# Modulation weights, and output weights for the samples' rows, multiplied as unsplit float32, four tiles in a row in four column groups

## The chip, the cores and the metric

The kernel runs on one core of a Trainium2 chip. A time is the device time of one execution in microseconds (us); the run before gave 2041.84 us as the median of three, from 2039.24 to 2042.91. The profile is of one further execution, of 2031.15 us. The engines are named as in its rows: PE (TensorE, matmuls), PEld (its weight loads), DVE (VectorE), ACT (ScalarE), POOL (GpSimd), SP (the queue that issues the transfers).

## The reference, cut to what matters

One layer of a streaming encoder is applied to a prompt of 1024 rows and to a sample of 32 rows, with 2048 channels. Two products matter here:

```python
shift, scale, gate = jnp.split(c @ w_mod + b_mod, 3, axis=-1)   # c: one row for the prompt, one for the sample
u = layer_norm(x) * (1.0 + scale[:, None]) + shift[:, None]
...                                                             # w_in, four branches of heads
o = jnp.concatenate([y_a, y_b, y_c, y_d], axis=-1) @ w_out      # 2048 x 2048
x_new = layer_norm(ALPHA * x + (1.0 + gate[:, None]) * o) * ln_g + ln_b
```

`c @ w_mod` has two rows, over a matrix of 2048 x 4096 for scale and shift. `@ w_out` has 1024 prompt rows and 32 sample rows.

## The kernel before, in words

Large products are made of float32 numbers split in two: a rounded high part (`float32r`, ACT's copy) and the rest (DVE's subtraction). A product is then three matmuls: high by high, high by low, low by high. The matmuls that take float32 as it is appear in the trace as two rows of PE each.

**Modulation.** `mod_group(g, part)` computes 512 of the columns of scale (part 1) or shift (part 0): 16 tiles `wmr` of 128x512 (256 KB each) are loaded, ACT casts each to `wmh` (L206), DVE subtracts (L207; POOL takes every fifth), and PE multiplies `wmh` by `cspl`, four columns that hold the high and the low parts of the two rows of `c` (L208), and `wml` by two of them (L209), all into one PSUM tile `mod`. DVE copies that tile (`mr`, L213), and four small matmuls (L215) add the rows that belong together and turn them into columns. Of eight such groups the first four (part 1) come first, since the scaled input `u` needs them: `build_u0` makes 16 tiles `uh`, `ul` from the transposed, normalised `x` (L273 to L279). The other four run woven with four column tiles of the input projection (`col_tile`, L337 to L339), which need `u`.

**The samples' rows in the output projection.** `out_proj(0)` handles the first 512 prompt rows and the 32 sample rows, in four blocks of 512 output columns. For each block eight weight tiles `wr` (2 of the 16 k each, 512 KB) are loaded (L308, two buffers), cast and subtracted to `wh`, `wl` (L312, L313, three buffers each). 24 matmuls of 512 columns multiply them by the prompt rows (`product`, L1218 to L1220). Then four matmuls (L1262, L1263) multiply the same `wh`, `wl` by the sample rows `ys` into `accs`. `so` (L1273) and one matmul (L1275) add the parts.

A scheduler fixes the order of each engine's instructions when the program is built; `tc.high_priority()` marks work that it puts as early as it can. Within an engine's queue, and in SP's, instructions are taken in that order.

Two other places serve as comparisons. `products` multiplies two heads j = 0, 1, which lie in partitions 0 to 63 and 64 to 127, so that their matmuls use different rows of the array. `values` multiplies unsplit float32 and puts the two heads in output partitions 0 to 63 and 64 to 127, that is in two column groups of the array:

```python
T.matmul(out, x[0], y[0], start=start, stop=False)      # products(), L716, called for j = 0, then for j = 1
T.matmul(out, x[0], y[1], start=False, stop=False)      # L717
T.matmul(out, x[1], y[0], start=False, stop=stop)       # L718
...
for j in range(2):                                       # values(), L829
    T.matmul(pa[64 * j:64 * j + 64, 0:P], vv[:, b * P + 64 * j:b * P + 64 * j + 64],
             wt[:, j * P:(j + 1) * P], start=first and b == 0, stop=last and b == m // P - 1,
             skip_group_check=True)
```

Of the kernel before, what the change touches and what calls it, by code (L numbers as in the profile page):

```python
# [62 lines left out]
def step_kernel(ctx, tc, xp, xs, cst, wmss, wmg, bgate, win, wsm, wout, lng, lnb, ck, cv,  # L63
# [72 lines left out]
    for sel, (s0, s1) in ((sel1, (0, 16)), (sel2, (32, 48))):  # L136
# [12 lines left out]
    A.activation(mulc, C("ral"), AF.Exp)  # L149
    V.tensor_scalar(mulc, mulc, -1.0, None, op0=ALU.mult)  # L150

    cspl = cp.tile([P, KD, 4], F32R, name="cspl")
    cT = g4(C("cT", 0, 32), KD)
    A.copy(cspl[:, :, 0:2], cT)
    V.tensor_tensor(cspl[:, :, 2:4], cT, cspl[:, :, 0:2].bitcast(F32), op=ALU.subtract)
    sel4 = cp.tile([4, 2], F32, name="sel4")
    tmp4 = cp.tile([4, 2], F32, name="tmp4")
    G.affine_select(out=sel4, in_=ones[0:4, 0:2], pattern=[[-1, 2]], compare_op=ALU.is_equal,
                    fill=0.0, base=0, channel_multiplier=1)
    G.affine_select(out=tmp4, in_=ones[0:4, 0:2], pattern=[[-1, 2]], compare_op=ALU.is_equal,  # L160
                    fill=0.0, base=-2, channel_multiplier=1)
    G.tensor_tensor(sel4, sel4, tmp4, op=ALU.add)


    mhi = cp.tile([6, 1], F32, name="mhi")
# [5 lines left out]
    sel32 = cp.tile([64, 32], F32, name="sel32")  # L171
    G.tensor_tensor(sel32, ident[0:64, 0:32], ident[0:64, 32:64], op=ALU.add)


    shiftH = cp.tile([P, KD, 2], F32R, name="shiftH")
# [19 lines left out]
    usc = dp.tile([KD, P, 512], F32, name="usc")  # L195
    gpk = [dp.tile([4, P, 544], F32, name=f"gpk{h}") for h in range(2)]


    def mod_group(g, part):
        o = ZT("mod")  # L200
        for kk in range(KD):
            wr = IO("wmr")
            nc.sync.dma_start(wr[:, 0:512], wmss[g, kk, part])
            wh = wk.tile([P, 512], F32R, tag="wk", name=nm("wmh"))
            wl = wk.tile([P, 512], F32R, tag="wk", name=nm("wml"))
            A.copy(wh, wr[:, 0:512])  # L206
            (G if kk % 5 == 4 else V).tensor_tensor(wl, wr[:, 0:512], wh.bitcast(F32), op=ALU.subtract)  # L207
            T.matmul(o[0:4], cspl[:, kk, :], wh, start=(kk == 0), stop=False, skip_group_check=True)  # L208
            T.matmul(o[0:2], cspl[:, kk, 0:2], wl, start=False, stop=(kk == KD - 1), skip_group_check=True)  # L209
            yield 1  # L210
        pc = ST("modc")
        mr = WK("mr")
        V.tensor_copy(mr[0:4, 0:512], o[0:4])  # L213
        for j in range(4):
            T.matmul(pc[:, 2 * j:2 * j + 2], mr[0:4, j * P:(j + 1) * P], sel4, start=True, stop=True)  # L215
        ks = slice(4 * g, 4 * g + 4)
        if part == 1:
            V.scalar_tensor_tensor(scale1[:, ks, :], g4(pc[:, 0:8], 4), 1.0,
                                   C("bmod", 16 + 4 * g, 4).to_broadcast([P, 4, 2]), op0=ALU.add, op1=ALU.add)
        else:  # L220
            sh = SM(8, "shf")
            V.tensor_tensor(g4(sh, 4), g4(pc[:, 0:8], 4), C("bmod", 4 * g, 4).to_broadcast([P, 4, 2]), op=ALU.add)
            V.tensor_copy(shiftH[:, ks, :], g4(sh, 4))
# [81 lines left out]
    def split_w(src, shape, pool=None):  # L305

        wr = wp.tile(shape, F32, tag="wr", name=nm("wr"), bufs=2)
        nc.sync.dma_start(wr, src)  # L308
        p, th, tl = (pool, "io", "io") if pool else (wp, "wh", "wl")
        wh = p.tile(shape, F32R, tag=th, name=nm("wh"))  # L310
        wl = p.tile(shape, F32R, tag=tl, name=nm("wl"))
        A.copy(wh, wr)  # L312
        V.tensor_tensor(wl, wr, wh.bitcast(F32), op=ALU.subtract)  # L313
        return wh, wl

    def spans(h, shift):

# [4 lines left out]
    def col_tile(h, tid, shift=None):  # L322

        if shift is None:
            shift = h == 0
        src = win[tid]
        with tc.high_priority():
            w = [split_w(src[:, q * 1024:(q + 1) * 1024].rearrange("p (a b) -> p a b", a=8), [P, 8, P])
                 for q in range(2)]
        res = []  # L330
        sp_ = spans(h, shift)
        for i, (c0, t0, o, n) in enumerate(sp_):
            pt = ps_ip.tile([P, 512], F32, tag="ip", name=nm("ip"))
            for k in range(KD):
                uh, ul = U[h, k]
                wh, wl = w[k // 8]
# [820 lines left out]
    def load_y(h, k):  # L1157
# [12 lines left out]
        A.copy(yh[:, 0:n], yf[:, 0:n])  # L1170
        V.tensor_tensor(yl[:, 0:n], yf[:, 0:n], yh[:, 0:n].bitcast(F32), op=ALU.subtract)
        if h == 0:
            if k % 8 == 0:
                YS[k // 8] = io.tile([P, 8, 64], F32R, tag="io", name=nm("ys2"))
            t = YS[k // 8]
            G.tensor_copy(t[:, k % 8, 0:32], yh[:, 512:544].bitcast(F32))
            G.tensor_copy(t[:, k % 8, 32:64], yl[:, 512:544].bitcast(F32))
        Y[h, k] = (yh, yl)

    def row_norm(st, m):  # L1180
# [9 lines left out]
    def out_proj(h):  # L1190
# [4 lines left out]
        for c0, w in blocks:  # L1195
# [12 lines left out]
            def weights(k0, n, pool=None):  # L1208
                src = wout[b, k0 // 4, :, :].rearrange("p (a b) -> p a b", a=4)[:, k0 % 4:k0 % 4 + n, o:o + w]
                with tc.high_priority():  # L1210
                    wh, wl = split_w(src, [P, n, w], pool)
                return [(k0 + i, wh[:, i, :], wl[:, i, :]) for i in range(n)]

            def product(t, ws, first, last):
                c = slice(t * P, (t + 1) * P)
# [38 lines left out]
            for kq in range(KD // nk):  # L1254
                ws = weights(kq * nk, nk)
                for t in range(4):
                    product(t, ws, kq == 0, kq == KD // nk - 1)
                if h == 0:
# [6 lines left out]
                    if b == 3:  # L1265
                        for k, _, _ in ws:
                            load_y(1, k)
                yield 1
            for t in range(4):
                residual(t, P, xp, h * 512 + t * P, acc[t][:, 0:w], gb[0])  # L1270
            if h == 0:
                so = WK("so")
                A.copy(so[0:64, 0:512], accs[0:64])  # L1273
                pt = ST("pso")
                T.matmul(pt[0:SMP, :], sel32[0:64], so[0:64, 0:512], start=True, stop=True)  # L1275
                residual(4, SMP, xs, 0, pt[0:SMP, :], gb[1])

    def finish0():
# [266 lines left out]
```

## Time and profile before

| | |
|---|---|
| median of three runs | 2041.84 us (2039.24 to 2042.91) |
| profiled execution | 2031.15 us |
| its span, first to last instruction | 2029.3 us |
| PE busy | 1941.8 us (96%) |
| DVE busy | 1426.9 us (70%) |
| ACT busy | 836.1 us (41%) |
| mean granted TensorE clock | 0.994 of full speed |

The span is what the rows below divide; 1.9 us of the profiled execution lie outside it. Matmuls overlap in the pipeline, so a matmul's own duration is longer than the time by which it holds back the next one: what a matmul costs is read from the starts of rows that follow each other.

### The profile page before, as it was taken

The page shows a single profiled execution, that of the slowest core. Times are in us where ns is not written, and L with a number is a line of the kernel's source. Part 1 is how long each engine was busy: PE and PEld are TensorE (multiplying, and loading weights), DVE is VectorE, ACT ScalarE, POOL GpSimd, SP SyncE. Part 2 cuts the span into 40 slices and gives each one's busy share as a digit, 9 for nine tenths or more (in the row PEclk, how much of TensorE's full clock was granted, in tenths as well). Part 3 has the DMA queues.
Part 4 walks back from the last instruction along what each step waited for, and adds up shares of the span by engine and source line. Part 5 has one row for each costly group of instructions (what it writes and reads, how often), then busy time and mean ns, then how long its engine had stood idle before and what let it go on. Part 6 is the DMA issues. An engine that isn't in the chain of part 4 may idle for free.

```text
span 2029.3 us, 31738 instructions
## 1 busy us (share of the span) xinstructions
PE 1941.8 (96%) x11820; PEld 1625.0 (80%) x11820; DVE 1426.9 (70%) x2713; ACT 836.1 (41%) x1407; POOL 323.8 (16%) x521
## 2 busy tenths in 40 slices
PE   2999999999999999999999999999999999999998
PEld 0568999998889999987787877777778777777787
DVE  6976558779776776877669797886757754356765
ACT  6663443333545434444444443534335521133321
POOL 1232011122121311241101010111102410000000
PEclk9999999999999999999999999999999999999999
DMA  9785334443444334364232333233342725468733
GB/s 306 250 281 185 107 119 131 127 137 102 139 132 137 110 106 120 85 204 141 91 114 95 119 92 108 82 110 113 106 120 92 224 94 168 128 224 261 229 126 130
DMA packets 162034, 291.40 MB, mean 144 GB/s; under 512 B 23836, under 2 KB 66076, under 8 KB 161880
## 3 DMA queue, kind: packets, MB, share of 16 engines
q1 hardware_dynamic: 161880, 289.37, 45.0%
q8 instruction: 93, 1.52, 0.3%
q14 instruction: 61, 0.50, 0.1%
HBM read 253.49 MB, written 35.82 MB: 143 GB/s over the span
## 4 chain that ended last, share of the span: by engine, by line
PE 53%; DVE 11%; DMA 4%; issue 4%; POOL 1%; ACT 1%; SPq 0%; POOLq 0%; DVEq 0%; ACTq 0%
PE ip L337 10%; PE ip L339 10%; PE ip L338 10%; PE op L1220 5%; PE op L1219 4%; PE op L1218 4%; DVE cv L1089 3%; DVE wl L313 2%; DMA val<-rsc 1%; DVE pr L697 1%; DMA wg<-in_wmg_dram 1%; PE av L829 1%; PE wt L814 1%; DVE gacc L1142 1%; ACT wh L312 1%
## 5 line engine op out<-in xcount | busy, mean ns | idle before, releaser
L337 PE MATMUL ip<-uh,wh 128*128 128x272 f32 (+4 forms) x2368 | 774.0, 328 | 0.6 <-DVE uh L278 0.6
L338 PE MATMUL ip<-ul,wh 128*128 128x272 f32 (+4 forms) x2368 | 764.6, 323 | 0.2
L339 PE MATMUL ip<-uh,wl 128*128 128x272 f32 (+4 forms) x2368 | 763.0, 322 | 0.0
L312 ACT CAST wh<-wr 128x1024 fp32r<-128x1024 f32 (+1 forms) x257 | 268.3, 1045 | 658.0 <-PE ip L338 379.8
L337 PEld LDWEIGHTS ip<-uh,wh 128*128 128x128 f32 x2368 | 449.2, 190 | 39.1 <-issue 5.5
L313 DVE TENSOR_TENSOR wl<-wr,wh 128x1024 fp32r<-128x1024 f32 (+1 forms) x257 | 315.0, 1226 | 233.7 <-ACT wh L312 221.7
L338 PEld LDWEIGHTS ip<-ul,wh 128*128 128x128 f32 x2368 | 450.1, 190 | 34.4 <-issue 2.4
L339 PEld LDWEIGHTS ip<-uh,wl 128*128 128x128 f32 x2368 | 449.8, 190 | 34.4 <-issue 2.0
L1218 PE MATMUL op<-wh,yh 128*128 128x512 f32 (+1 forms) x576 | 214.0, 372 | 3.1 <-DVE val L1229 3.1
L1219 PE MATMUL op<-wl,yh 128*128 128x512 f32 (+1 forms) x576 | 213.4, 371 | 0.0
L1220 PE MATMUL op<-wh,yl 128*128 128x512 f32 (+1 forms) x576 | 212.6, 370 | 0.0
L1089 DVE SCALAR_TENSOR_TENSOR cv<-cin,cs,cv 128x574 f32<-128x574 f32 (+1 forms) x240 | 187.5, 781 | 2.9
L1218 PEld LDWEIGHTS op<-wh,yh 128*128 128x128 f32 x576 | 108.3, 188 | 26.7 <-DVE val L1229 4.0
L1219 PEld LDWEIGHTS op<-wl,yh 128*128 128x128 f32 x576 | 108.3, 188 | 22.0 <-issue 2.6
L1220 PEld LDWEIGHTS op<-wh,yl 128*128 128x128 f32 x576 | 108.3, 188 | 20.8 <-issue 1.3
L790 POOL TENSOR_SCALAR_AFFINE_SELECT s<-s 128x128 f32<-128x128 f32 x64 | 36.3, 568 | 430.2 <-ACT s L688 430.0
L1142 DVE SCALAR_TENSOR_TENSOR gacc<-wg,cs,gacc 128x512 f32<-128x512 f32 x120 | 89.2, 760 | 17.7 <-DMA wg<-in_wmg_dram 17.4
L208 PE MATMUL mod<-wmh,cspl 128*4 128x512 f32 x128 | 52.9, 413 | 34.6 <-ACT wmh L206 34.5
L207 DVE TENSOR_TENSOR wml<-wmr,wmh 128x512 fp32r<-128x512 f32 x104 | 78.9, 812 | 3.9 <-ACT wmh L206 3.2
L206 ACT CAST wmh<-wmr 128x512 fp32r<-128x512 f32 x128 | 71.0, 621 | 15.4 <-PE modc L215 10.3
L697 DVE TENSOR_TENSOR_SCAN pr<-kp 128x128 f32<-128x128 f32 (+4 forms) x66 | 54.0, 818 | 14.4 <-POOL kp L792 11.7
L688 ACT ACTIVATE s<-z 128x512 f32<-128x512 f32 (+3 forms) x96 | 47.7, 497 | 34.9 <-PE z L718 33.1
(382 smaller groups left out, 2504.2 us busy)
## 6 DMA issues: line engine op xcount, KB each, us to landing
wr<-in_win_dram SPq DMA_DIRECT2D x192, 512.0 KB
wmr<-in_wmss_dram SPq DMA_DIRECT2D x128, 256.0 KB
wr<-in_wout_dram SPq DMA_DIRECT2D x63, 512.0 KB
wg<-in_wmg_dram SPq DMA_DIRECT2D x64, 256.0 KB
x<-in_xp_dram SPq DMA_DIRECT2D x32, 256.0 KB
out_dram<-val SPq DMA_DIRECT2D x32, 256.0 KB
xr<-in_xp_dram SPq DMA_DIRECT2D x28, 256.0 KB
yf<-ysc SPq DMA_DIRECT2D x16, 272.0 KB
```

Source lines behind the costliest of these rows:

```text
L207: (G if kk % 5 == 4 else V).tensor_tensor(wl, wr[:, 0:512], wh.bitcast(F32), op=ALU.subtract)
L312: A.copy(wh, wr)
L313: V.tensor_tensor(wl, wr, wh.bitcast(F32), op=ALU.subtract)
L337: T.matmul(pt[:, 0:n], wh[:, k % 8, :], uh[:, c0:c0 + n], start=(k == 0), stop=False)
L338: T.matmul(pt[:, 0:n], wh[:, k % 8, :], ul[:, c0:c0 + n], start=False, stop=False)
L339: T.matmul(pt[:, 0:n], wl[:, k % 8, :], uh[:, c0:c0 + n], start=False, stop=(k == KD - 1))
L697: V.tensor_tensor_scan(pr[0:rows, 0:nk][:, ::-1], kp[0:rows, 0:nk][:, ::-1], kp[0:rows, 0:nk][:, ::-1], initial=init, op0=ALU.mult, op1=AL ...
L1089: V.scalar_tensor_tensor(acc[:, 0:n], t[:, i:i + n], C("cdw", 31 * j + i), acc[:, 0:n], op0=ALU.mult, op1=ALU.add)
L1142: V.scalar_tensor_tensor(acc[j][:, 0:512], wr[:, 0:512], cT[:, k, j:j + 1], acc[j][:, 0:512], op0=ALU.mult, op1=ALU.add)
L1218: T.matmul(acc[t][:, 0:w], yh[:, c], wh, start=(first and i == 0), stop=False)
L1219: T.matmul(acc[t][:, 0:w], yh[:, c], wl, start=False, stop=False)
L1220: T.matmul(acc[t][:, 0:w], yl[:, c], wh, start=False, stop=(last and i == len(ws) - 1))
```

## The change

The modulation tiles are no longer cast and subtracted. Four of them are loaded, and four matmuls take them as they are, each with 32 columns of an unsplit, padded copy of `c` (`cpad`), of which the first two count; matmul i writes partitions 32 i to 32 i + 31 of `mod`, that is column group i of the array. `behind` keeps the four in a row, the one whose tile was loaded last in front. `mr` and the small matmuls now take 128 rows, with a selection `sel2c` that adds the four groups.

In `out_proj(0)` the sample rows `YS` are kept unsplit in one tile (POOL copies, 16 in place of 32). Each weight tile `wr` (two k) meets them as it is, in four matmuls of 256 columns: two k by two halves of the 512 columns, in four column groups. They are issued with the loading of the tile, at high priority, and no longer behind the products; `wr`'s buffer is thus held until they have read it. `sel64` adds the groups, in two matmuls of 256 columns.

```diff
-        for kk in range(KD):
-            wr = IO("wmr")
-            nc.sync.dma_start(wr[:, 0:512], wmss[g, kk, part])
-            wh = wk.tile([P, 512], F32R, tag="wk", name=nm("wmh"))
-            wl = wk.tile([P, 512], F32R, tag="wk", name=nm("wml"))
-            A.copy(wh, wr[:, 0:512])
-            (G if kk % 5 == 4 else V).tensor_tensor(wl, wr[:, 0:512], wh.bitcast(F32), op=ALU.subtract)
-            T.matmul(o[0:4], cspl[:, kk, :], wh, start=(kk == 0), stop=False, skip_group_check=True)
-            T.matmul(o[0:2], cspl[:, kk, 0:2], wl, start=False, stop=(kk == KD - 1), skip_group_check=True)
+
+        for kq in range(4):
+            ws = []
+            for i in range(4):
+                wr = IO("wmr")
+                nc.sync.dma_start(wr[:, 0:512], wmss[g, 4 * kq + i, part])
+                ws.append(wr)
+                if i < 3:
+                    yield 1
+
+            with tc.high_priority():
+                after = None
+                for i in (3, 0, 1, 2):
+                    c0 = 2 * (4 * kq + i)
+                    mm = T.matmul(o[32 * i:32 * i + 32], cpad[:, c0:c0 + 32], ws[i][:, 0:512], start=(kq == 0),
+                                  stop=(kq == 3), skip_group_check=True)
+                    after = behind(mm, after)
             yield 1
...
-        V.tensor_copy(mr[0:4, 0:512], o[0:4])
+        V.tensor_copy(mr[:, 0:512], o)
         for j in range(4):
-            T.matmul(pc[:, 2 * j:2 * j + 2], mr[0:4, j * P:(j + 1) * P], sel4, start=True, stop=True)
+            T.matmul(pc[:, 2 * j:2 * j + 2], mr[:, j * P:(j + 1) * P], sel2c, start=True, stop=True)
...
-            if k % 8 == 0:
-                YS[k // 8] = io.tile([P, 8, 64], F32R, tag="io", name=nm("ys2"))
-            t = YS[k // 8]
-            G.tensor_copy(t[:, k % 8, 0:32], yh[:, 512:544].bitcast(F32))
-            G.tensor_copy(t[:, k % 8, 32:64], yl[:, 512:544].bitcast(F32))
+            if k == 0:
+                YS[0] = io.tile([P, KD, SMP], F32, tag="io", name=nm("ys2"))
+            G.tensor_copy(YS[0][:, k, :], yf[:, 512:544])
...
                 with tc.high_priority():
-                    wh, wl = split_w(src, [P, n, w], pool)
+                    wh, wl, wr = split_w(src, [P, n, w], pool)
+                    if h == 0:
+                        sample(k0, wr)
                 return [(k0 + i, wh[:, i, :], wl[:, i, :]) for i in range(n)]
+
+            def sample(k0, wr):
+
+                after = None
+                for i in range(4):
+                    k, x = k0 + i // 2, i % 2
+                    mm = T.matmul(accs[32 * i:32 * i + 32, 0:256], YS[0][:, k, :], wr[:, i // 2, x * 256:(x + 1) * 256],
+                                  start=(k0 == 0), stop=(k0 == KD - 2), skip_group_check=True)
+                    after = behind(mm, after)
...
-                    for k, wh, wl in ws:
-                        ys = YS[k // 8][:, k % 8, :]
-                        T.matmul(accs[0:64], ys, wh, start=(k == 0), stop=False, skip_group_check=True)
-                        T.matmul(accs[0:32], ys[:, 0:32], wl, start=False, stop=(k == KD - 1),
-                                 skip_group_check=True)
```

On PE, in the second modulation group, the matmuls `mod` stood singly between those of the column tiles `ip`, each behind ACT's, DVE's or POOL's split of its tile:

```order
L209 MATMUL mod_417<-wml_467,cspl 2x512 [waits Pool_49]
L208 MATMUL mod_417<-wmh_474,cspl 4x512 [waits Activation_49]
L338 MATMUL ip_1064<-ul_451,wh_1054 128x272 [waits DVE_49]
L339 MATMUL ip_1064<-uh_450,wl_1055 128x272
L209 MATMUL mod_417<-wml_475,cspl 2x512 [waits DVE_49]
L208 MATMUL mod_417<-wmh_482,cspl 4x512 [waits Activation_49]
```

At the same place PE has now, with the new line numbers (L351 to L353 are the old L337 to L339):

```order
L353 MATMUL ip_817<-uh_349,wl_734 128x272
L289 MATMUL xt_108_470<-ident,x_257 128x32 [waits Activation_49]
L221 MATMUL mod_336<-wmr_369,cpad 32x512 [waits DMAHW1_49]
L221 MATMUL mod_336<-wmr_363,cpad 32x512 [waits DMAHW6_49]
L221 MATMUL mod_336<-wmr_365,cpad 32x512 [waits DMAHW7_49]
L221 MATMUL mod_336<-wmr_367,cpad 32x512 [waits DMAHW0_49]
L352 MATMUL ip_743<-ul_402,wh_733 128x272 [waits DVE_49]
```

Eight matmuls in eight places became four in one place, and these wait for the transfers of their tiles themselves.

On PE in the output projection, in a later block, the samples' matmuls stood behind the 24 products of their own weight tile:

```order
L1219 MATMUL op_18138<-wl_18143,yh_17137 128x512
L1220 MATMUL op_18138<-wh_18142,yl_17138 128x512
L1262 MATMUL ops_18139<-wh_18142,ys_3086_17132 64x512 [waits PE_49]
L1263 MATMUL ops_18139<-wl_18143,ys_3086_17132 32x512
L1262 MATMUL ops_18139<-wh_18142,ys_3086_17132 64x512
L1263 MATMUL ops_18139<-wl_18143,ys_3086_17132 32x512
L1218 MATMUL op_18135<-wh_18176,yh_17145 128x512
```

Now four of them (the first of them has a row of its own, the other three share one) stand among the products of the weight tile four places earlier; here behind 23 of the 24 products of tile `wr_17333`, for tile `wr_17518`, which is the fourth after it:

```order
L1242 MATMUL op_17153<-wl_17336,yh_16585 128x512
L1233 MATMUL ops_17483<-wr_17518,ys_2830_16491 32x256 [waits DMAHW6_49]
L1233 MATMUL ops_17483<-wr_17518,ys_2830_16491 32x256 x3
L1243 MATMUL op_17153<-wh_17335,yl_16586 128x512
L1241 MATMUL op_17150<-wh_17369,yh_16592 128x512
```

They moved ahead by some four products' sets, and what they wait for is now the transfer of a weight tile that is not multiplied until later.

## Rows read from the trace of the kernel before

**Rows 1.** The page: span, busy time by engine, granted clock by slice.
```profile
span 2029.3 us, 31738 instructions
...
PE 1941.8 (96%) x11820; PEld 1625.0 (80%) x11820; DVE 1426.9 (70%) x2713; ACT 836.1 (41%) x1407; POOL 323.8 (16%) x521
...
PEclk9999999999999999999999999999999999999999
```
**Rows 2.** Windows: start:end, length, busy us per engine, clock, DMA share, GB/s.
```profile
33.00:101.00 68.00, 61.30 (x314) 34.42 (x314) 59.98 (x83) 47.33 (x92) 18.40 (x12) 1.00 0.83 270
101.00:183.00 82.00, 76.68 (x468) 55.39 (x468) 58.94 (x83) 47.16 (x87) 32.23 (x36) 0.98 0.66 225
1580.00:1830.00 250.00, 247.56 (x1097) 189.46 (x1096) 133.68 (x214) 74.62 (x108) 30.86 (x45) 1.00 0.53 172
```
**Rows 3.** Timeline of DVE: start, us, engine, line, idle before; groups 1, 4, 8 end.
```profile
47.43 0.68 DVE L213 COPY mr<-mod 4x512 f32<-4x512 f32 x1 [0.81 <-PE mod L209]
...
100.70 0.68 DVE L213 COPY mr<-mod 4x512 f32<-4x512 f32 x1 [0.58 <-PE mod L209]
...
182.72 0.68 DVE L213 COPY mr<-mod 4x512 f32<-4x512 f32 x1 [0.48 <-PE mod L209]
```
**Rows 4.** Instructions that read the tile wmr: ns min/median/max, first and last start.
```profile
L206 ACT CAST wmh<-wmr x128: 600/621/651, 32.0 to 180.0; 128x512 fp32r<-128x512 f32 x128
L207 DVE TENSOR_TENSOR wml<-wmr,wmh x104: 670/684/1786, 32.7 to 180.6; 128x512 fp32r<-128x512 f32 x104
```
**Rows 5.** Waits from 0 to 200 us: total, times, longest (SP's, then all).
```profile
SPq L203 <- DVE wml L207: 35.6, 50, 2.9
SPq L308 <- DVE wl L313: 35.0, 9, 16.0
...
PEld mod L209 <- DVE wml L207: 12.8, 24, 1.4
```
**Rows 6.** Timeline of PE at 63 us: two split matmuls of 512 columns.
```profile
62.95 0.40 PE L208 MATMUL mod<-wmh,cspl 128*4 128x512 f32 x1
63.18 0.39 PE L209 MATMUL mod<-wml,cspl 128*2 128x512 f32 x1
```
**Rows 7.** Timeline of PE at 522 us: unsplit float32, two rows a matmul.
```profile
522.23 1.02 PE L939 MATMUL pq<-cv,wq 128*128 128x512 f32 x2
523.10 1.02 PE L942 MATMUL pk<-cv,wq 128*128 128x512 f32 x2
```
**Rows 8.** Timeline of PE at 1017 us: row halves, then two column groups.
```profile
1016.54 0.50 PE L716 MATMUL z<-prevh,qh 64*128 64x512 f32 x2
1016.88 0.40 PE L717 MATMUL z<-prevl,qh 64*128 64x512 f32 x2
1017.11 0.41 PE L718 MATMUL z<-prevh,ql 64*128 64x512 f32 x2
1017.45 1.09 PE L829 MATMUL av<-wt,prev 128*64 128x128 f32 x16
1018.47 0.77 PE L814 MATMUL wt<-ident,s 128*128 128x128 f32 x5
```
**Rows 9.** Timeline of PE at 1674 us: one set of samples' matmuls begins and has ended.
```profile
1674.44 0.39 PE L1262 MATMUL ops<-wh,ys 128*64 128x512 f32 x1
...
1675.36 0.40 PE L1218 MATMUL op<-wh,yh 128*128 128x512 f32 x1
```
**Rows 10.** Timelines of ACT and SP there: cast of a weight tile, the next load.
```profile
1675.37 1.05 ACT L312 CAST wh<-wr 128x1024 fp32r<-128x1024 f32 x1 [5.01 <-issue]
...
1677.70 0.33 SPq L308 DMA_DIRECT2D wr<-in_wout_dram  x1
1678.90 2.10 SPq L1235 DMA_DIRECT2D rsc<-val  x2
```
**Rows 11.** Timelines of SP and ACT at the start: two weight loads, the first cast.
```profile
0.81 0.87 SPq L308 DMA_DIRECT2D wr<-in_win_dram  x2
...
4.60 1.04 ACT L312 CAST wh<-wr 128x1024 fp32r<-128x1024 f32 x1 [2.51 <-DMA wr<-in_win_dram]
```

More of the change, by code (lines that the diff above doesn't have):

```diff
@@ L150, in step_kernel @@
     V.tensor_scalar(mulc, mulc, -1.0, None, op0=ALU.mult)
-    cspl = cp.tile([P, KD, 4], F32R, name="cspl")
     cT = g4(C("cT", 0, 32), KD)
[L154 to L162, printed above, removed]
+    cpad = cp.tile([P, 2 * KD + 30], F32, name="cpad")
+    V.memset(cpad[:, 2 * KD:], 0.0)
+    V.tensor_copy(cpad[:, 0:2 * KD], C("cT", 0, 32))
+    sel2c = cp.tile([P, 2], F32, name="sel2c")
+    G.tensor_tensor(sel2c, ident[:, 0:2], ident[:, 32:34], op=ALU.add)
+    G.tensor_tensor(sel2c, sel2c, ident[:, 64:66], op=ALU.add)
+    G.tensor_tensor(sel2c, sel2c, ident[:, 96:98], op=ALU.add)
     mhi = cp.tile([6, 1], F32, name="mhi")
@@ L169, in step_kernel @@
     V.tensor_scalar(mlo, mhi, -1.0, 1.0, op0=ALU.mult, op1=ALU.add)
-    sel32 = cp.tile([64, 32], F32, name="sel32")
-    G.tensor_tensor(sel32, ident[0:64, 0:32], ident[0:64, 32:64], op=ALU.add)
+    sel64 = cp.tile([P, 64], F32, name="sel64")
+    G.tensor_tensor(sel64, ident[:, 0:64], ident[:, 64:128], op=ALU.add)
     shiftH = cp.tile([P, KD, 2], F32R, name="shiftH")
@@ L196, in step_kernel, with behind @@
     gpk = [dp.tile([4, P, 544], F32, name=f"gpk{h}") for h in range(2)]
+    def behind(ins, other):
+        if other is not None:
+            tc.add_manual_dep(ins.ins, other.ins.name, mybir.DependencyInfo(
+                mybir.DependencyClass.NoSync, mybir.DependencyReason.DATA), reason="order")
+        return ins
     def mod_group(g, part):
         o = ZT("mod")
-        for kk in range(KD):
-            wr = IO("wmr")
-            nc.sync.dma_start(wr[:, 0:512], wmss[g, kk, part])
-            wh = wk.tile([P, 512], F32R, tag="wk", name=nm("wmh"))
-            wl = wk.tile([P, 512], F32R, tag="wk", name=nm("wml"))
-            A.copy(wh, wr[:, 0:512])
-            (G if kk % 5 == 4 else V).tensor_tensor(wl, wr[:, 0:512], wh.bitcast(F32), op=ALU.subtract)
-            T.matmul(o[0:4], cspl[:, kk, :], wh, start=(kk == 0), stop=False, skip_group_check=True)
-            T.matmul(o[0:2], cspl[:, kk, 0:2], wl, start=False, stop=(kk == KD - 1), skip_group_check=True)
+        for kq in range(4):
[13 more added lines that the diff above has]
+                    after = behind(mm, after)
             yield 1
@@ L313, in split_w @@
         V.tensor_tensor(wl, wr, wh.bitcast(F32), op=ALU.subtract)
-        return wh, wl
+        return wh, wl, wr
     def spans(h, shift):
@@ L335, in col_tile @@
                 uh, ul = U[h, k]
-                wh, wl = w[k // 8]
+                wh, wl, _ = w[k // 8]
                 T.matmul(pt[:, 0:n], wh[:, k % 8, :], uh[:, c0:c0 + n], start=(k == 0), stop=False)
@@ L1257, in out_proj @@
                     product(t, ws, kq == 0, kq == KD // nk - 1)
-                if h == 0:
-                    for k, wh, wl in ws:
-                        ys = YS[k // 8][:, k % 8, :]
-                        T.matmul(accs[0:64], ys, wh, start=(k == 0), stop=False, skip_group_check=True)
-                        T.matmul(accs[0:32], ys[:, 0:32], wl, start=False, stop=(k == KD - 1),
-                                 skip_group_check=True)
-                    if b == 3:
-                        for k, _, _ in ws:
-                            load_y(1, k)
+                if h == 0 and b == 3:
+                    for k, _, _ in ws:
+                        load_y(1, k)
                 yield 1
@@ L1272, in out_proj @@
                 so = WK("so")
-                A.copy(so[0:64, 0:512], accs[0:64])
+                A.copy(so[:, 0:256], accs[:, 0:256])
                 pt = ST("pso")
-                T.matmul(pt[0:SMP, :], sel32[0:64], so[0:64, 0:512], start=True, stop=True)
+                for x in range(2):
+                    T.matmul(pt[0:SMP, x * 256:(x + 1) * 256], sel64[:, 32 * x:32 * x + 32], so[:, 0:256],
+                             start=True, stop=True)
                 residual(4, SMP, xs, 0, pt[0:SMP, :], gb[1])
```

## The prediction, on record before the run

> **What bounds the kernel now.** I read the page first. The span is 2029.3 us and PE is busy for 1941.8 us of it, 96%, at full clock in every slice [rows 1]: nearly everywhere a microsecond of PE work is a microsecond of the span. The start is another matter. So the second view is that of the windows, cut at the ends of the modulation groups [rows 3]: group 1 ends at 47.43, group 4 at 100.70, group 8 at 182.72 us. From 33 to 101 us DVE is busy for 59.98 of 68 us and the DMA engines at a share of 0.83; from 101 to 183 us PE has 76.68 of 82 us, DVE 58.94, DMA 0.66 [rows 2]. The waits say what ties these together: PE's weight loads wait for DVE's split 24 times, SP's loads of `wmr` wait 50 times, 35.6 us in all, for the same split, because it holds the tile's buffer [rows 5]. So modulation part 1 (four groups) is bound by the splitting on DVE and ACT, close above the transfers; part 2 by PE, with little to spare. In the output projection (1580 to 1830 us) PE has 247.56 of 250 us [rows 2]: bound by PE.
>
> **The cost of a set of four.** Before, a split matmul of 512 columns holds PE for 0.23 us [rows 6], so four tiles cost 8 x 0.23 = 1.84 us, and four samples' matmuls 0.92 us [rows 9]. Unsplit float32 alone takes 0.87 us for 512 columns, two passes of 0.435 [rows 7]: four of these one after another would be 3.48 us. What four column groups do no row shows; the nearest rows have two. The 16 passes `av` of 128 columns, 0.109 us each by the rate of [rows 7], would take 1.74 us one after another and 0.87 us two at a time; the next work begins 1.02 us after their start [rows 8]. So two groups do run at once, at an extra of 0.15 us. At the entry `av` begins 0.34 us behind the pair before it, where 0.23 is the pair's due (1016.88 to 1017.11): 0.11 us more [rows 8]. I put 0.26 us on each set for both turns. With four at once a set costs 2 x 0.435 + 0.26 = 1.13 us, for the samples (256 columns, passes of 0.218 us) 2 x 0.218 + 0.26 = 0.70 us. The bounds are none at once, 3.74 and 2.00 us, and four at once with the turns hidden, 0.87 and 0.44 us. I take four at once, since the nearest row has every group that was filled working. PE's work falls by 32 x 0.71 = 22.7 us for the modulation and by 32 x 0.22 = 7.0 us for the samples.
>
> **Order within a set.** The program gives each matmul's two passes one behind the other, so the second pass must be overtaken by the next group's first. The six matmuls z are issued as L716, L717, L718 for one head and then for the other, and the trace has them in pairs, L716 twice, L717 twice, L718 twice [rows 8]: the array does let one part run ahead of another. The Trainium skill, page "TensorE: Matmul & The Clock Gate", Part 3, says otherwise: matmuls start and end strictly in program order, and only weight loads are pulled ahead. By that rule a set would take five passes in place of two. The rows z speak against it; I keep it as a rival.
>
> **The start, to 183 us.** The change takes away 128 casts of 0.621 us on ACT and 104 subtractions of 0.684 us on DVE [rows 4], 71 us of DVE's 119 in these windows. Then DVE no longer bounds part 1. Next is the transfer: 16 tiles are 4.19 MB; 270 GB/s at a share of 0.83 make 325 GB/s when full [rows 2], so 12.9 us a group. Now a group takes (100.70 - 47.43) / 3 = 17.8 us [rows 3]. I take 14 us: the floor and 1.1 us for the chain `mr`, L215, scale, `u`, during which PE has transposes. The first group now waits for casts; without them it ends when its tiles are there, which I put at 41 us. Part 1 then ends at 41 + 3 x 14 = 83 us, 18 us earlier. Part 2 has 82 us, of which the 16 sets give back 16 x 0.71 = 11.4; its transfers, 225 GB/s over 82 us, would need 57 us, so they don't bind. I take 12 us. Sum: -30 us. If part 1 kept its pace it would be -11; with both parts at the transfers' floor (41 + 38.7 + 57 = 137 us) it would be -46.
>
> **The samples.** The PE saving is 7.0 us. Against it stands a new wait: the set stands in PE's queue ahead of products and waits for the transfer of its `wr` tile. The chain is this: a set of 24 products ends and frees a `wh` buffer; ACT casts and DVE subtracts, which frees a `wr` buffer; SP issues the next load 2.33 us after the cast began (1675.37 to 1677.70) [rows 10]; it lands 3.8 us later if it takes as long as two did at the start (0.81 to 4.60) [rows 11]. That is 6.1 us after the products' end. PE reaches the set after 23 products and a set (23 x 0.231 + 0.70 = 6.0 us) at about half the places, after 26 (6.7 us) at the others. So the waits are near nothing at 3.8 us, and some 35 us in all if a load takes 1.5 us longer. Everything behind the set on PE waits with it, and PE is the bound here. I take +5 us for all; the samples then bring -2 us.
>
> **The rest.** The copy `mr` now has 128 rows in place of 4, with the same 512 columns; whether it grows no row shows, but 8 such copies of 0.68 us [rows 3] lie beside PE's transposes, and doubling them would cost 5 us at most if nothing hid them. `so` has half the columns. The two last matmuls have as many columns as the one before. The constants (`cpad`, `sel2c`, `sel64`) are made while the first tiles load. POOL loses 16 copies and is busy for 16% [rows 1]. None of it is counted.
>
> **Sum.** -30 - 2 = -32 us, 1999 us for the profiled execution of 2031.15. The median of the three runs lies 10.7 us above that execution; I keep this distance: 2010 us.
>
> **Rivals.** First, that a set does not run four wide. (a) Passes strictly in order, by the skill's rule as above: a set takes 5 x 0.435 + 0.26 = 2.44 us, a samples' set 1.35. Part 2 loses 16 x 0.60 = 10 us, the samples 32 x 0.43 = 14 and some 5 of waits, while part 1, no longer bound by PE or DVE, still gains some 16: +13, so 2055 us. (b) Two at once and no more, for want of ways to feed four streams: 2.00 and 1.13 us a set; part 2 +2.6, samples +6.7 and 4 of waits, part 1 -17: -4, so 2038 us. (c) One at a time, 3.74 and 2.00 us: 61 + 35 us more, less some 10 from the freed DVE: 2128 us. For (b) and (c) speaks only that no row has four groups; against (a) and (c) speak the rows z and `av`.
>
> Second, on the other side: the samples' sets wait for their transfers. SP takes its queue in order, and a load can stand behind stores of `rsc` that wait for DVE, 2.1 us in one row [rows 10]. If each load lands 2 us later than I assumed, PE stands 28 times for about 1.8 us, 50 us in all, against gains of 37: +13, 2055 us. It decides from 37 / 32 = 1.2 us a set on. Against it: before, loads were issued long ahead of their cast, and half of the sets have 0.6 us to spare.
>
> Third, the start hardly gains: SP's queue also holds the loads of the column tiles, which wait for their buffers, up to 16 us at once [rows 5], and `wmr` loads stand behind them. PE's saving in part 2 and nothing in part 1 is left, -12: 2030 us.
>
> **How the numbers follow.** I call within 0.2% (4 us) no change, about what a measurement of this kernel can tell. The forecast has a chance of 0.64, its own range is 1990 to 2030. Rival (a) 0.08, (b) 0.06, (c) 0.05, the samples' waits 0.10, the start without gain 0.07. Faster are the forecast, the third rival and a part of (b): 0.73; same 0.07; slower 0.20. The range goes from 1988 (the floor of -46, and the samples' saving kept) to 2050, which leaves out (c) and the larger part of (a) and of the waits, and so holds about 0.8.
>
> **What would show it.** Rows L221 in fours with starts within some 0.02 us, and the next row 1.0 to 1.2 us after the first: four wide. Starts at 0.43 us steps: (a) or (c). The fourth L227 copy of `mr` near 83 us in place of 100.70, and the eighth near 153, with a DMA share over 0.9 in part 1. In the output projection idle time of PE ahead of L1233 that ended with the DMA of `wr`: under 10 us in all by the forecast, 40 or more by the second rival. The forecast is wrong if part 1 keeps 17 us a group although DVE is idle, or if the sets of L1233 take their saving back.

## The result, and the profile after

The changed kernel takes 2014.57 us (median of four runs, 2011.09 to 2018.59), the kernel before, on the same chip, 2040.54 us (2034.1 to 2042.91): ratio 0.9883, 95% interval 0.9863 to 0.9904, a gain of 26 us by the medians. The profiled execution took 2011.09 us, 20.1 less than that of before.

The page of the changed kernel, beside [rows 1]:

```profile
span 2009.2 us, 31503 instructions
...
PE 1916.5 (95%) x11956; PEld 1599.0 (80%) x11956; DVE 1341.6 (67%) x2610; ACT 767.0 (38%) x1278; POOL 272.7 (14%) x481
```

The copies `mr` on DVE, groups 1, 2, 3, 4 and 8, beside [rows 3]:

```profile
40.29 0.69 DVE L227 COPY mr<-mod 128x512 f32<-128x512 f32 x1 [7.53 <-PE mod L221]
57.41 0.69 DVE L227 COPY mr<-mod 128x512 f32<-128x512 f32 x1 [6.39 <-PE mod L221]
71.66 0.69 DVE L227 COPY mr<-mod 128x512 f32<-128x512 f32 x1 [1.58 <-PE mod L221]
85.89 0.69 DVE L227 COPY mr<-mod 128x512 f32<-128x512 f32 x1 [6.70 <-PE mod L221]
...
165.93 0.69 DVE L227 COPY mr<-mod 128x512 f32<-128x512 f32 x1 [7.44 <-PE mod L221]
```

Groups 2, 3 and 4 of part 1 take 17.1, 14.2 and 14.2 us, 15.2 in the mean in place of 17.8. In the first of these the granted clock is at half for 6.8 us, from 41.5 us on. DVE now stands idle for 1.6 to 7.5 us right ahead of each of these copies. The copy of 128 rows takes 0.69 us, that of 4 took 0.68. Window of part 1, from the first copy to the fourth:

```profile
41.00:86.60 45.60, 42.50 (x288) 27.22 (x288) 17.13 (x31) 11.68 (x25) 0.00 (x0) 0.93 0.82 290
```

PE is busy for 42.5 of 45.6 us there and the DMA engines at a share of 0.82: while PE waits for modulation tiles, it does work of the column tiles. What the whole start is worth is seen at the first matmul `ipn` behind all modulation, at 220.3 us before and 190.5 after. Windows up to that instruction, the kernel before (columns as in [rows 2]):

```profile
0.00:220.30 220.30, 175.58 (x1072) 127.03 (x1073) 160.51 (x264) 122.64 (x222) 57.88 (x88) 0.99 0.74 243
```

and the changed kernel:

```profile
0.00:190.50 190.50, 150.45 (x1072) 110.66 (x1073) 74.34 (x155) 55.06 (x93) 11.65 (x64) 0.97 0.82 280
```

The same 1072 records on PE; its busy time fell by 25.1 us, its idle time by 4.7: 29.8 us.

Timeline of PE at 60 us, a set and the next instruction:

```profile
60.74 1.07 PE L221 MATMUL mod<-wmr,cpad 128*32 128x512 f32 x8
61.74 0.55 PE L287 MATMUL xt<-ident,x 128*128 128x128 f32 x3
```

All matmuls L221 that started from 60.70 to 61.00 us (count, ns min/median/max, first and last start):

```profile
L221 PE MATMUL mod<-wmr,cpad x4: 617/617/618, 60.7 to 60.8; 128*32 128x512 f32 x4
```

Timeline of PE at 101 us, a set with its neighbours:

```profile
101.37 0.29 PE L351 MATMUL ip<-uh,wh 128*128 128x272 f32 x1
101.59 1.06 PE L221 MATMUL mod<-wmr,cpad 128*32 128x512 f32 x8
102.58 0.39 PE L352 MATMUL ip<-ul,wh 128*128 128x272 f32 x1
102.81 0.29 PE L353 MATMUL ip<-uh,wl 128*128 128x272 f32 x1
```

Eight passes (x8) of 0.6 us each fit in 1.07 us. The first passes of all four matmuls start together (single starts 60.741, 60.748, 60.755 and 60.761 us), the second ones together at 61.20. A second pass has been overtaken by three first ones: in the trace only a matmul's second record raises a semaphore, and here the four records that raise one come last, while in the run below in which the sets have one column group every second record does, which is the order of the queue. From L351 to L353 pass 1.44 us, where two steps of 0.126 us would be due: a set holds PE for 1.19 us, with both turns (the median of 14 such sets is 1.19, too).

The same for a set of samples:

```profile
1704.18 0.40 PE L1243 MATMUL op<-wh,yl 128*128 128x512 f32 x1
1704.51 0.64 PE L1233 MATMUL ops<-wr,ys 128*32 128x256 f32 x8
1705.08 0.50 PE L1241 MATMUL op<-wh,yh 128*128 128x512 f32 x1
1705.41 0.39 PE L1242 MATMUL op<-wl,yh 128*128 128x512 f32 x1
```

From L1243 to L1242 pass 1.23 us, less two products of 0.231: 0.77 us a set, against 0.92 [rows 9]. So 32 sets save 4.8 us. Yet the first product of the output projection starts 29.6 us earlier than before and the last one only 20.1. The products of the high parts, before and after (first and last start):

```profile
L1218 PE MATMUL op<-wh,yh x576: 274/392/797, 1601.5 to 2014.5; 128*128 128x512 f32 x150, 128*128 128x256 f32 x42
```

```profile
L1241 PE MATMUL op<-wh,yh x576: 274/393/799, 1571.9 to 1994.4; 128*128 128x512 f32 x150, 128*128 128x256 f32 x42
```

The output projection lost 9.5 us. Its waits on PE (total, times, longest):

```profile
PE op L1241 <- DVE val L1252: 7.6, 2, 6.7
PE ops L1233 <- DMA wr<-in_wout_dram: 4.7, 5, 2.2
```

The second row is the wait that the prediction priced at 5 us. The first has grown; before, the same accumulators were waited for 3.1 us in all:

```profile
PE op L1218 <- DVE val L1229: 3.1, 2, 1.6
```

The 6.7 us stand at 1851 us, ahead of the 978th product, behind the samples' last set. Timeline of ACT there:

```profile
1852.03 2.23 ACT L1308 ACTIVATE val<-val,ors 128x512 f32<-128x512 f32 x3 [9.49 <-DMA val<-rsc]
1854.17 1.03 ACT L326 CAST wh<-wr 128x1024 fp32r<-128x1024 f32 x1
```

Of DVE:

```profile
1855.23 1.22 DVE L327 TENSOR_TENSOR wl<-wr,wh 128x1024 fp32r<-128x1024 f32 x1 [7.13 <-ACT wh L326]
...
1856.97 0.68 DVE L1252 TENSOR_TENSOR val<-op,gb 128x512 f32<-128x512 f32 x1
```

And of PE:

```profile
1857.71 0.79 PE L1241 MATMUL op<-wh,yh 128*128 128x512 f32 x1 [6.70 <-DVE val L1252]
```

Three activations of `finish0` wait for their rows from memory; behind them on ACT stands the cast of a weight tile, behind that on DVE its subtraction, and behind that the multiplication that empties an accumulator, for which PE waits.

The kernel before has the same succession on ACT and DVE ahead of the same product, but there its rows came sooner. Its first activation, and the product:

```profile
1872.61 0.82 ACT L1290 ACTIVATE val<-val,ors 128x512 f32<-128x512 f32 x1 [4.01 <-DMA val<-rsc]
```

```profile
1878.56 0.50 PE L1218 MATMUL op<-wh,yh 128*128 128x512 f32 x1 [1.51 <-DVE val L1229]
```

SP's reads of these rows, before and after:

```profile
1866.93 1.54 SPq L1289 DMA_DIRECT2D val<-rsc  x3
```

```profile
1844.05 2.11 SPq L1307 DMA_DIRECT2D val<-rsc  x3
```

The 961st product starts 26.0 us earlier than before (1846.90 for 1872.94), but these reads are issued only 22.9 us earlier, and the first activation behind them starts only 20.6 us earlier. So the order of ACT and DVE at this place is that of before, and the rows come 5.5 us later against the products. Already the first read of `rsc` is 1.8 us late in this sense (1837.9 and 1813.7 us); why SP issues them later was not tested.

Behind this wait the clock is at half, too:

```profile
1857.70:1860.50 2.80, 2.79 (x7) 2.21 (x8) 2.80 (x5) 0.00 (x0) 0.00 (x0) 0.50 0.80 245
```

Windows of the changed kernel in the first block of the output projection:

```profile
1592.00:1604.00 12.00, 8.82 (x49) 5.89 (x47) 5.50 (x17) 3.08 (x8) 4.54 (x4) 1.00 0.25 78
1604.00:1607.00 3.00, 3.00 (x14) 2.52 (x15) 0.85 (x3) 0.00 (x0) 0.00 (x0) 0.64 0.81 262
```

PE was idle for 3.2 of 12 us, and then the granted clock is 0.64 for 3 us. Before, no window of 4 us there had less than 1.00, though PE idled there for 2.4 us.

### The profile page after: what moved, and what is told of

Same layout as the page of the kernel before. It is cut to its first block, busy times and chain, and to the rows that moved or that the text cites. A ratio compares the mean times of both kernels' runs of the same rounds, so it can differ in the third digit from the quotient of the medians.

```text
span 2009.2 us, 31503 instructions
## 1 busy us (share of the span) xinstructions
PE 1916.5 (95%) x11956; PEld 1599.0 (80%) x11956; DVE 1341.6 (67%) x2610; ACT 767.0 (38%) x1278; POOL 272.7 (14%) x481
## 5 line engine op out<-in xcount | busy, mean ns | idle before, releaser
L351 PE MATMUL ip<-uh,wh 128*128 128x272 f32 (+4 forms) x2368 | 775.8, 328 | 0.4 <-POOL uh L277 0.4
L353 PE MATMUL ip<-uh,wl 128*128 128x272 f32 (+4 forms) x2368 | 764.1, 323 | 0.0
L351 PEld LDWEIGHTS ip<-uh,wh 128*128 128x128 f32 x2368 | 449.5, 190 | 38.9 <-issue 7.7
L353 PEld LDWEIGHTS ip<-uh,wl 128*128 128x128 f32 x2368 | 449.3, 190 | 37.7 <-issue 7.3
L1243 PE MATMUL op<-wh,yl 128*128 128x512 f32 (+1 forms) x576 | 215.4, 375 | 0.0
L1242 PE MATMUL op<-wl,yh 128*128 128x512 f32 (+1 forms) x576 | 214.4, 372 | 0.0
L1243 PEld LDWEIGHTS op<-wh,yl 128*128 128x128 f32 x576 | 109.0, 189 | 26.4 <-issue 7.3
L1242 PEld LDWEIGHTS op<-wl,yh 128*128 128x128 f32 x576 | 108.8, 189 | 22.3 <-issue 3.0
L1156 DVE SCALAR_TENSOR_TENSOR gacc<-wg,cs,gacc 128x512 f32<-128x512 f32 x120 | 89.1, 760 | 17.1 <-DMA wg<-in_wmg_dram 17.0
L221 PE MATMUL mod<-wmr,cpad 128*32 128x512 f32 x256 | 38.2, 674 | 34.0 <-DMA wmr<-in_wmss_dram 34.0
L715 DVE TENSOR_TENSOR s<-s,pr 128x512 f32<-128x512 f32 (+5 forms) x106 | 59.5, 564 | 2.0
L514 DVE SCALAR_TENSOR_TENSOR cv<-cin,cs,cv 128x547 f32<-128x547 f32 (+1 forms) x72 | 55.2, 767 | 0.3
```

The source lines that it names most:

```text
L514: V.scalar_tensor_tensor(acc[:, 0:n], t[:, i:i + n], C(wname, j * tap + i), acc[:, 0:n], op0=ALU.mult, op1=ALU.add)
L715: V.tensor_tensor(s[0:rows, 0:m], s[0:rows, 0:m], pr[0:rows, 1:m + 1], op=ALU.mult)
L1156: V.scalar_tensor_tensor(acc[j][:, 0:512], wr[:, 0:512], cT[:, k, j:j + 1], acc[j][:, 0:512], op0=ALU.mult, op1=ALU.add)
L1242: T.matmul(acc[t][:, 0:w], yh[:, c], wl, start=False, stop=False)
L1243: T.matmul(acc[t][:, 0:w], yl[:, c], wh, start=False, stop=(last and i == len(ws) - 1))
```

## The experiments

Two theories of the loss in the output projection: **A**, the samples' change causes it by the place of its sets and by the order of other engines' work around them; **B**, any shift of the program by 30 us would, since transfers then meet other transfers.

**One part alone.** The modulation change alone (`sample` taken out, L1262 and L1263 of before put back):

> The modulation change alone; the samples' rows are multiplied as in the kernel before. Theory A (the loss behind the start comes from the samples' change): the first product of the output projection starts 29.5 to 30.5 us earlier than before, and the last product too, so the span is 1998 to 2001 us, 8 to 11 us less than with both parts. Theory B (the loss comes with the shift of the whole program by 30 us, whatever the samples do): the first product is 30 us early, the last one only 20 to 23 us, span 2006 to 2009 us.

The samples' change alone:

> The samples' change alone, modulation as before. Theory A: the start is that of before within 1 us, and the output projection takes 5 to 11 us longer, with waits of L1233's sets for the transfer of their weight tile of 4 to 8 us in all: span 2034 to 2040 us. Theory B: the samples' saving of about 8 us on PE less 4 to 8 us of waits is left: span 2024 to 2030 us.

Measured: the modulation alone 2005.5 us, ratio 0.9852 (0.9837 to 0.9867); the samples alone 2044.7 us, ratio 1.0045 (1.0031 to 1.0058), slower than before. The products of the high parts with the modulation alone (L1232 there):

```profile
L1232 PE MATMUL op<-wh,yh x576: 274/393/792, 1576.4 to 1988.9; 128*128 128x512 f32 x150, 128*128 128x256 f32 x42
```

It ends 25.7 us earlier than before and begins 25.1 us earlier: the output projection lost nothing, so B falls. The span, 2003.7 us, lies above the expected 1998 to 2001. (The first `ipn` was at 190.5 us, 29.8 earlier; 4.8 us went on the way there, where this execution has stretches under full clock from 216 to 220 and from 476 to 484 us that the changed kernel has not: two times 3.4 us at half clock, worth some 3.4 of the 4.8.) With the samples alone, PE's waits in the output projection:

```profile
PE op L1234 <- DVE val L1245: 8.9, 3, 5.6
PE ops L1226 <- DMA wr<-in_wout_dram: 7.0, 4, 2.9
```

Both waits are there without any shift of the start. The profiled execution lost 15 us in the output projection, more than the 5 to 11 expected, and its span of 2046.2 us lies above the 2034 to 2040. At the 978th product PE waits 5.6 us with the samples alone and 1.4 with the modulation alone, 6.7 with both and 1.5 before: this wait, too, comes with the samples' change.

How the runs stand to before, product by product (start of the n-th product `op`, in order of starts, less that of before, in us; the first column is the first `ipn`):

| run | `ipn` | 1st | 97th | 769th | 1681st |
|---|---|---|---|---|---|
| changed kernel | -29.8 | -29.6 | -23.4 | -26.1 | -20.0 |
| modulation alone | -29.8 | -25.1 | -25.2 | -25.2 | -25.6 |
| samples alone | +0.1 | +1.8 | +11.5 | +8.9 | +16.9 |
| set at its own tile | -30.2 | -30.2 | -25.5 | -31.4 | -22.1 |
| emptying first | -28.7 | -24.3 | -11.5 | -14.6 | -18.3 |
| own tile, emptying first | -29.6 | -25.8 | -20.7 | -26.7 | -28.1 |
| modulation alone, emptying first | -31.0 | -28.1 | -27.9 | -27.9 | -19.2 |

Between the first two columns these kernels do the same work; I put the differences there down to such stretches, which no run tests. Of what a kernel with early sets loses up to the 97th product, about 3 us come back up to the 193rd (in the changed kernel 6.2 and -3.2), since PE has done some later work by then: over the whole first block (192 products) it loses 3.0 us. The samples' sets lie between the 1st and 769th product; `finish0`, woven with the second half of the rows, behind the 769th.

**The place of a set.** `sample` is issued behind the loading, without the priority, and so stands ahead of the 24 products of its own tile:

```diff
-                    if h == 0:
-                        sample(k0, wr)
+                if h == 0:
+                    sample(k0, wr)
                 return [(k0 + i, wh[:, i, :], wl[:, i, :]) for i in range(n)]
```

> Both parts, but a set of samples' matmuls stands right ahead of the 24 products of its own weight tile, not two to four tiles earlier; the buffer of the tile is held that much longer. If the sets' place costs the time (theory A): no set waits for a transfer (under 1 us in all), and the span is 1991 to 1998 us, the 30 us of the start and 4 to 8 of the samples. Rival: the longer hold delays the next weight tile, the wait moves to the products behind the splits, and the span stays at 2005 to 2012 us.

2007.82 us, ratio 0.9859 (0.9844 to 0.9873), its span of 2007.2 outside what I expected and inside the rival's range. The longest of its waits from 1560 us on:

```profile
PE op L1241 <- DVE val L1252: 8.0, 3, 5.4
```

No set waits for a transfer any more, and the rival's wait behind the splits is in no row: the longer hold of the buffer costs nothing that the waits show. From the 1st to the 769th product this kernel gains 1.2 us on before where the changed kernel loses 3.5. So the place did cost 4.7 us; the wait for the emptying is another matter and has stayed (5.4 us at the 978th product).

**The order on DVE.** The emptying multiplication is marked as high priority:

```diff
-                V.tensor_tensor(val, oin, g[0:m, 0:w], op=ALU.mult)
+                with tc.high_priority():
+                    V.tensor_tensor(val, oin, g[0:m, 0:w], op=ALU.mult)
```

alone, then with the set at its own tile, then, as a control, with the samples as before:

> The changed kernel, with the multiplication that empties a product's accumulator (L1252 there) marked as high priority, so that it no longer stands behind a split on DVE that waits for ACT. If the 6.7 us that PE waits near 1851 us come from this order (theory: ACT's cast of a weight tile stands behind three activations that wait for transfers, DVE's split behind the cast, the emptying behind the split): that wait falls under 2.5 us, the step at that place from 6.6 to under 2 us, and the span to 2000 to 2005 us. Rival (the transfers themselves are late, and the next one waits for them in turn): the wait moves to the products behind the split, span 2007 to 2011 us.

> A set of samples' matmuls right ahead of the products of its own tile, and the emptying of the accumulators at high priority. If both causes are what they seem, both waits are gone: first product 30 us earlier than before, last one 28 to 32 us earlier, span 1996 to 2001 us. Rival as for the run with the emptying alone: span 2004 to 2009 us.

> The modulation change alone, samples as before, and the emptying of the accumulators at high priority: the control for the sets at their own tile with the same priority (ratio 0.9813). If the samples' change is worth its 32 x 0.25 = 8 us of PE time once its two waits are gone, this kernel is 4 to 8 us slower than that one, 2003 to 2008 us by the runs' medians. Rival (the priority alone made the gain): 1997 to 2002 us.

Medians and ratios: 2009.62 us, 0.9862 (0.9843 to 0.9881); 1999.22 us, 0.9813 (0.9798 to 0.9828); the control 2010.37 us, 0.9866 (0.9842 to 0.9889). In the first of them the wait of 7.6 us is gone (no wait of PE for `val` of an accumulator is among the waits shown, the wait for `wr` is):

```profile
PE ops L1233 <- DMA wr<-in_wout_dram: 6.6, 6, 3.0
```

and from the 769th to the last column it gains 3.7 us on before where the changed kernel loses 6.1; its span (2011.0) is at the end of the rival's range, but the rival's wait behind the split isn't there: the time was lost earlier, where the table shows it. In this run the rows of `finish0` came sooner, too (ACT waits 2.6 us for them there), so it does not tell the emptying's place from the rows' lateness. With both, only 1.9 us are left of that wait, none for `wr`; the span of 2001.1 us is at the end of what I expected, the first product 25.8 us early, not 30:

```profile
PE op L1241 <- DVE val L1253: 1.9, 1, 1.9
```

Of the kernels that leave nothing out this is the fastest of the study. But the control, with the same priority and the old samples, lies 2 us above its expected range, 11 behind this kernel, and has a longer wait than before:

```profile
PE op L1232 <- DVE val L1244: 9.2, 2, 5.7
```

So the priority is no cure by itself: with the old samples it moves the wait to other products (3.5 us at the 961st, 5.7 at the 1153rd). How `finish0`, whose activations wait for rows, meets the casts and emptyings decides over up to 9 us there, and an edit elsewhere can change it. Against the modulation alone without the priority (0.9852), the samples' part and the priority together bring 8 us; how much of it is luck in that meeting is not separated, and so the 11 us to the control are not the samples' worth.

**The first block.** Six of the eight sets there left out (from the fastest kernel); then the control with less split work and no column groups in that block:

> Sets at their own tile and the priority, but in the first block of the output projection only two of eight sets of samples' matmuls (six are left out). The first 96 products took 4.4 to 4.8 us longer with the sets there than before, with a stretch at half clock. If the sets themselves cost the clock: no stretch under full clock between 1570 and 1620 us, and a step of -5 to -2 us over these products. Rival (PE reaches the older work of the branches sooner, waits there, and the clock falls after the wait): the fall stays, and the step is -1 to +2 us.

> The modulation change alone with the priority; in the first block the samples' matmuls with the low parts are left out but for the last (15 of 16), so that PE has 3.5 us less work there and no column groups. If the sets in column groups cost the clock: full clock between 1570 and 1620 us and a step over the first 96 products of -2 to -0.5 us. Rival (arriving sooner costs it): a stretch at half clock, as in the kernels with the sets, and a step of 0 to +3 us.

One execution each (2002.65 and 2020.34 us). Without sets in column groups, but with 3.5 us less PE work, the windows are:

```profile
1590.00:1600.00 10.00, 7.27 (x32) 5.25 (x30) 5.47 (x11) 5.24 (x9) 6.26 (x11) 0.97 0.49 157
1600.00:1606.00 6.00, 5.91 (x18) 5.05 (x19) 1.75 (x5) 0.37 (x2) 0.04 (x1) 0.50 0.14 41
```

2.7 us idle, then half clock; over the first 96 products the execution lost 3.8 us on before, of which 1.4 come back up to the 193rd, with 3.5 us less to do in the block. With two sets left the fall stayed too (0.50 from 1592 to 1600 us), and the step was -0.2 us. The run with half of the loads (below) has all eight sets in the block and full clock there. So the clock falls without the sets, and with them it need not fall. In the rows the falls stand behind waits of PE for POOL, in the last work of the branches (`py`, `pst`). But how much PE idles does not settle it. Here are ten us of the kernel before, of the run with one group, and of the run with the set at its own tile, the last with the 6.5 us that follow:

```profile
1618.00:1628.00 10.00, 7.56 (x40) 5.48 (x39) 4.48 (x13) 2.44 (x6) 4.28 (x4) 1.00 0.35 105
```

```profile
1660.50:1670.50 10.00, 7.09 (x41) 5.01 (x41) 4.87 (x14) 2.67 (x6) 3.23 (x4) 1.00 0.07 21
```

```profile
1580.50:1590.50 10.00, 8.20 (x41) 5.59 (x39) 6.28 (x13) 6.42 (x11) 3.82 (x5) 1.00 0.73 207
1590.50:1597.00 6.50, 6.47 (x20) 5.41 (x21) 3.15 (x8) 0.47 (x2) 0.41 (x1) 0.50 0.01 1
```

PE idled for 2.4 and 2.9 us in the first two, and no stretch under full clock followed in the block; it idled for 1.8 in the third, and the clock fell to half. What makes it fall is open.

**How many at once.** All four modulation matmuls into the same 32 partitions, or into two column groups in turn:

```diff
-                    mm = T.matmul(o[32 * i:32 * i + 32], cpad[:, c0:c0 + 32], ws[i][:, 0:512], ...
+                    mm = T.matmul(o[0:32], cpad[:, c0:c0 + 32], ws[i][:, 0:512], ...
```

> As the changed kernel, but the four modulation matmuls of a set all write the same 32 partitions (one column group). If the four groups are what lets them run together: eight passes of 0.435 us, 3.5 to 3.8 us from a set's first row to the next work in place of 1.0, and 32 sets x 2.6 = 83 us more PE work, of which up to 20 hide in waits for transfers at the start: span 2070 to 2095 us. Rival (matmuls of 32 columns overlap anyway): sets of 1.0 to 2 us and a span under 2040 us.

> As the changed kernel, but the four modulation matmuls of a set go to two column groups in turn (two matmuls for each). If groups run together and matmuls of one group follow each other: starts in pairs, four steps of 0.435 us, 1.8 to 2.0 us from a set's first row to the next work in place of 1.0; 32 x 0.87 = 28 us more PE work, of which the 63 us of the run with one group for 83 us worked out let me expect 15 to 28 in the span: 2024 to 2037 us. Rival (strictly in program order, a pass that must wait for its group holds all behind it): 2.2 to 2.6 us a set.

One group: 2077.61 us; here four sets follow each other, 32 passes in 13.92 us, 0.435 each:

```profile
100.32 13.92 PE L221 MATMUL mod<-wmr,cpad 128*32 128x512 f32 x32
```

Two groups: 2038.21 us, 1.84 us from a set to the next row:

```profile
60.38 1.91 PE L221 MATMUL mod<-wmr,cpad 128*32 128x512 f32 x8
62.22 0.33 PE L287 MATMUL xt<-ident,x 128*128 128x128 f32 x1
```

Both as expected (one execution each). The first `ipn` came at 251.8 us with one group, 207.2 with two, 190.5 with four, against 220.3 before: without the groups the change would lose 31.5 us at the start, with two it gains 13.1.

**What bounds part 1 now.** Two of four tiles are loaded, and each is multiplied twice:

```diff
+                if i < 2:
+                    wr = IO("wmr")
+                    nc.sync.dma_start(wr[:, 0:512], wmss[g, 4 * kq + i, part])
+                    ws.append(wr)
+                else:
+                    ws.append(ws[i - 2])
```

> As the changed kernel, but only two of the four modulation tiles of a set are loaded, and each is multiplied twice (half of the modulation weights are left out). If transfers set the pace of part 1 (14.2 us a group, share 0.84): a group falls to 9 to 11 us, where PE's own work ends the gain, and the fourth copy mr comes at 60 to 72 us in place of 85.9. Rival (PE sets the pace, 44.8 of 50 us busy): the groups stay at 13 to 14.2 us, and only the first group, which waits for nothing but transfers, comes earlier, by 8 to 12 us: fourth copy at 74 to 78 us.

Timeline of DVE, the copies `mr` of part 1:

```profile
36.73 0.69 DVE L230 COPY mr<-mod 128x512 f32<-128x512 f32 x1 [2.48 <-PE mod L224]
...
63.19 0.68 DVE L230 COPY mr<-mod 128x512 f32<-128x512 f32 x1
```

8.8 us a group in place of 15.2, a little under the expected 9 to 11, and the fourth copy at 63.2 us: the loading sets the pace of part 1, as the prediction had it. Not all of it is the transfers themselves: in the changed kernel SP's loads of `wmr` also wait for sets that still hold their buffers, 12.4 us in all from 30 to 100 us. This run, which leaves out half of the loads, does not separate the two.

## Why the prediction was right, and where its terms were off

- **The set of four.** 1.13 us taken, 1.19 measured; 0.70 and 0.77 for the samples. The two passes of 0.435 us were right, and the turns cost 0.32 to 0.34 us in place of 0.26: 0.1 us at the entry and 0.12 to 0.13 at the end, as [rows 8] had it nearly, and the second product behind a set comes 0.10 us late too, which [rows 8] did not show. The savings were 32 x (1.84 - 1.19) = 20.8 us for 22.7, and 4.8 for 7.0.
- **Rival (a)**, passes strictly in order: refuted by the starts at 60.74 us and by both runs with fewer groups (1.84 us with two, where waiting passes would have made it 2.2 or more). The rows z, on which the prediction leaned, show pairs but not the order of the queue; the starts and the semaphores of the set do. The rule of the Trainium skill, page "TensorE: Matmul & The Clock Gate", Part 3, that matmuls start and end in program order, does not hold for the passes of different column groups here: a second pass waits while three later first passes start. Whether whole matmuls still end in order these rows cannot tell, since the four have one name. Rivals (b) and (c) fall by the same starts.
- **The start.** -30 us forecast, -29.8 measured at the first `ipn`, and the third rival (hardly any gain) falls. That the numbers agree so well is in part luck: the first group ended at 40.3 us for 41, part 1 at 85.9 for 83 (15.2 us a group for 14), so part 1 brought 14.8 us for 18, and what lies behind it 15.0 for 12. PE's busy time fell by 25.1 us, 4.3 more than the sets' price gives; where these come from is not shown. The DMA share in part 1 was 0.82, not over 0.9. The eighth copy came at 165.9 us, not 153: that mark was wrong, since PE does more of the column tiles' work ahead of the last group than before (496 rows `ip` for 386); that gain is seen only behind it.
- **The samples, the term that failed.** -2 us forecast, +9.5 in the profiled execution. The price of the wait for `wr` was right (5 us, 4.7 measured), the saving 2.2 us too high, so that the sets' waits took their saving back, which the prediction had named as a sign of being wrong. And two costs were missing: 6.6 us between the 961st and 1009th product, 5.2 of them a longer wait for the emptying, behind rows of `finish0` that come later, and about 1.4 at half clock behind it; and some 3 us in the first block, 1.4 of longer waits for POOL and 1.7 of a lower clock behind them. -4.8 + 4.7 + 6.6 + 1.4 + 1.7 = +9.6; 0.6 us come back behind the 1009th product, so the sum leaves some 0.5 us open, and it is that of one execution. That the 6.6 us come with the samples' change is shown by the runs with one part alone, and that they pass through the emptying by the waits. Why the rows come later, and what brings the clock down, is not shown.
- **The second rival** (sets waiting for their transfers) had the right mechanism at a tenth of its price.
- **From span to median.** The profile forecast was 12 us too low (1999 for 2011.09), the median only 4.6 us (2010 for 2014.57): the distance of 10.7 us that I kept from before was 3.5 here, and this offset most of the miss in the span. Here, too, the good number is luck.

## What to carry to other kernels

Few-row products in unsplit float32 pay when four of them fill four column groups in a row: price a set as its passes once, plus the turns on both sides. With two groups a set cost PE as much as the split had (1.84 us), and the start gained only 13.1 us. A set that reads a raw weight tile belongs where the tile has surely landed, right ahead of its own products, not at the loading. And an edit that is worth a few microseconds on PE can be outweighed by when other engines' work and transfers then come: compare, stage by stage, when the same instruction starts, before and after, and what it waited for.

## What the runs showed of the hardware that I had not expected

Less work on PE did not mean less time: in one execution PE idled for 2.7 us within 10 us, the granted clock then stood at 0.50 (1.2 GHz, the lower of its two levels) for the next 6 us, and the first block, with 3.5 us less to do, took 2.4 us longer than before. Turning to the column groups and back costs about 0.1 us on the instruction ahead, 0.12 to 0.13 at the set's end and 0.1 on the second one behind, nearly the same for sets of 512 and of 256 columns.
